# The last block product of a SwiGLU FFN with tokens as rows: residual and LayerNorm along the row, four tiles of 128 tokens

## The chip, the cores and the metric

One core of a Trainium2 chip runs one layer of a diffusion backbone. The metric is the device time of one execution in microseconds; the kernel before took 1520.83 us (median of three runs, 1520.49 to 1521.16). TensorE multiplies and transposes into PSUM, which has eight banks of 128 x 512 float32 values. VectorE (DVE) and ScalarE (ACT) read PSUM and SBUF, GpSimd (POOL) only SBUF, and SyncE (SP) issues most DMA transfers.

## The reference

All is float32. Ahead of the end, the layer computes modulated inputs, a windowed and a global attention, their merge, a first LayerNorm, and the up projection with its convolution and gate. The end, which the change rewrites, is the last two lines:

```
u = silu(gate) * val                       # 1024 tokens x 2816
y = u @ w_down                             # 2816 x 1024
x = alpha * x + gate2 * y                  # gate2: one factor per channel
mu  = mean(x, channels); var = mean((x - mu)^2, channels)
out = (x - mu) * rsqrt(var + 1e-5) * ln2_g + ln2_b
```

The mean and the variance of a token run over its 1024 channels; `gate2`, `ln2_g` and `ln2_b` belong to channels.

## The kernel before, in words

**Layout.** Channels lie on partitions: `zv(f, s)` is the tile of channels 128f to 128f+127 (f = 0 to 7) for a range `s` of tokens, and holds the residual `alpha * x`, to which the gated products are added. Sums over channels are then sums over partitions, which TensorE makes by a product with a column of ones (`onec`).

**Products.** Every float32 operand is split into a high and a low part; `mm3` issues three matmuls (high x high, low x high, high x low). The up and the down projection go by Strassen-Winograd's seven block products instead of eight. For the down projection, tokens 0 to 511 (`h0`) and 512 to 1023 (`h1`) and the two halves of channels and of the inner dimension are the blocks. `product(p)` makes the products p = 1, 6, 2, 7, 4, 5 in that order, each 4 blocks x 11 steps x 3 matmuls of 128 x 512 columns. `ev` and `accum` bring each result from PSUM into `zv`, with the factor `gain` (the gate, or its negative `nmod`).

**The last product, p = 3**, touches only channels 0 to 511 of tokens 512 to 1023. Its operands are the pairs `d3[k]` (k = 0 to 10): `[:, 0]` holds 512 columns of a weight combination, `[:, 1]` the 512 tokens of `h1`, each in a high part `h` and a low part `l`. `last_mm` makes it channel block by channel block with the weights stationary and tokens moving, 256 tokens at a time: first tokens 512 to 767 (`LN2_S[1]`), then 768 to 1023 (`LN2_S[2]`), 4 channel blocks each, so every matmul has 256 columns.

**The norm.** Tokens 0 to 511, and again 512 to 767, go through `ln_steps`: sums and squares by TensorE, the statistics, a broadcast by transposes (`cast`), and then per channel block `apply` and `emit2`, which stores the tile. `pend` holds these steps, and `tick` lets one out when enough matmuls have been issued. The last 256 tokens go another way: `prep` makes squares and `ln2_g`-scaled copies on ScalarE, and `tok(f)` issues on TensorE the sums of z, the transposes that bring channel block f of each 128 tokens into rows (`zt`), and the sums of squares. After the last `tok`, VectorE makes mean and variance (`mvl`, `rsl`, with a power on POOL), puts the mean on (L1813), then scale and shift (L1821; one of the four tiles by ScalarE and POOL, L1818 and L1819), and SP stores four tiles.

**What sets the order.** From the first LayerNorm on, TensorE's order is that of the program (`manual_schedule`); on the other engines a scheduler places instructions, save for VectorE after `win` is entered. A PSUM tile with the tag of an older one waits until the older one has been read. `yb` and `ab` are the two groups of four banks: `ab` holds the results of p = 5, `yb` is free by then.

**Output.** The output is `(8, 128, 1024)`, block, channel, token; for the last 256 tokens the rows are written as 512-byte pieces that hold 128 channels of one token, and the host puts these in place.

Of the kernel before, what the change touches and what calls it, by code (L numbers as in the profile page):

```python
# [70 lines left out]
def layer_kernel(  # L71
# [1659 lines left out]
    s = LN2_S[-1]
    w = s.stop - s.start
    nt = w // P

    def pst(n, name):
        return ps4.tile([P, HALF], F32, tag=f"r{n}", name=name)

    pr = [ht(f"pr{n}", (P, 4, w)) for n in range(4)]
    nc.vector.tensor_scalar(out=pr[0][:, 3, 0:P], in0=ident, scalar1=ln2c[:, 3:4], scalar2=None, op0=ALU.mult)
    nc.gpsimd.tensor_scalar(out=lnr[0], in0=lnr[0], scalar1=-1.0, scalar2=0.0, op0=ALU.mult, op1=ALU.add)  # L1740
    zt = {1: [pst(n, f"zt1_{n}") for n in ab[0:2]]}
    st = pst(ab[2], "stl")
    zero4 = post.tile([P, 8], F32, tag="zero4", name="zero4")
    nc.vector.memset(zero4, 0.0)

    def prep(f):
        nc.scalar.activation(pr[2 + f // 4][:, f % 4], zv(f, s), AF.Square)
        if f != 3:
            nc.scalar.activation(pr[f // 4][:, f % 4], zv(f, s), AF.Identity, scale=ln2c[:, f:f + 1])

    def tok(f):
        z, g = zv(f, s), pr[f // 4][:, f % 4]
        if f == 4:
            nc.tensor.matmul(st[:, 0:2 * nt], ident, zero4[:, 0:2 * nt], start=True, stop=True)
        for t in range(nt):
            ts = slice(t * P, (t + 1) * P)
            nc.tensor.matmul(st[:, t:t + 1], z[:, ts], onec, start=False, stop=True, skip_group_check=True)
        for t in range(nt):
            ts = slice(t * P, (t + 1) * P)
            o = zt[f // 4][t][:, (f % 4) * P:(f % 4 + 1) * P]  # L1760
            if f == 3:
                nc.tensor.matmul(o, z[:, ts], pr[0][:, 3, 0:P], start=True, stop=True)
            else:
                nc.tensor.transpose(o, g[:, ts], ident)
        for t in range(nt):
            ts = slice(t * P, (t + 1) * P)
            nc.tensor.matmul(st[:, nt + t:nt + t + 1], pr[2 + f // 4][:, f % 4, ts], onec, start=False, stop=True,
                             skip_group_check=True)
# [20 lines left out]
    zt[0] = [pst(n, f"zt0_{n}") for n in yb[0:2]]  # L1789
    pend += ln_steps(zs2, zq2, r, "b1", emit2, *LN2_E, LN2_P[1])  # L1790
    r = LN2_S[2]
    for f, done_ in enumerate(((7,), (0,), (1,), (2, 3))):
        o = pst(yb[2 + f % 2], f"yl{f}_{r.start}")[:, 0:w]
        last_mm(o, f, r, range(NH))
        accum(f, r, o, True)
        prep(f)
        for n in done_:
            tok(n)
# [2 lines left out]
    mv, m2, rs = sv
    drain(OTK)
    win = ctx.enter_context(ExitStack())
    win.enter_context(tc.manual_schedule(engines={mybir.EngineType.DVE}))
    nc.vector.tensor_scalar(out=mv, in0=st[:, 0:2 * nt], scalar1=1.0 / D, scalar2=None, op0=ALU.mult)
    nc.vector.tensor_tensor(out=m2[:, 0:nt], in0=mv[:, 0:nt], in1=mv[:, 0:nt], op=ALU.mult)
    nc.vector.scalar_tensor_tensor(out=rs[:, 0:nt], in0=mv[:, nt:2 * nt], scalar=LN_EPS, in1=m2[:, 0:nt],
                                   op0=ALU.add, op1=ALU.subtract)
    nc.gpsimd.tensor_tensor(out=rs[:, 0:nt], in0=rs[:, 0:nt], in1=mhalf[:, 0:nt], op=ALU.pow)
    ot = {}  # L1810
    for t, a in OTO:
        o = ot[t, a] = ht(f"ot{t}_{a}", (P, HALF))
        nc.vector.scalar_tensor_tensor(out=o, in0=lnr[0][:, a], scalar=mv[:, t:t + 1], in1=zt[a][t], op0=ALU.mult,  # L1813
                                       op1=ALU.add)
    for t, a in OTO:
        o = ot[t, a]
        if (t, a) in OTP:
            nc.scalar.activation(o, o, AF.Identity, scale=rs[:, t:t + 1])  # L1818
            nc.gpsimd.tensor_tensor(out=o, in0=o, in1=lnr[1][:, a], op=ALU.add)  # L1819
        else:  # L1820
            nc.vector.scalar_tensor_tensor(out=o, in0=o, scalar=rs[:, t:t + 1], in1=lnr[1][:, a], op0=ALU.mult,  # L1821
                                           op1=ALU.add)
        ts = slice(s.start + t * P, s.start + (t + 1) * P)
        nc.sync.dma_start(out[4 * a:4 * a + 4, :, ts].rearrange("f p q -> p f q"),
                          o.rearrange("p (f q) -> p f q", q=P))
# [89 lines left out]
def _assemble(got):  # L1915
    import numpy as np

    got = np.asarray(got)
    s = LN2_S[-1].start
    r = np.empty((T, KT, P), got.dtype)  # L1920
    r[:s] = got[:, :, :s].transpose(2, 0, 1)
    r[s:] = got[:, :, s:].reshape(KT, P, -1, P).transpose(2, 1, 0, 3).reshape(T - s, KT, P)
# [19 lines left out]
```

## Time and profile before

| | |
|---|---|
| median of three runs | 1520.83 us |
| profiled execution | 1520.56 us |
| its span | 1518.7 us |
| mean granted clock of TensorE | 0.997 |
| TensorE busy | 1500.7 us, 99% |
| VectorE busy | 1166.4 us, 77% |
| ScalarE busy | 789.0 us, 52% |
| GpSimd busy | 757.3 us, 50% |
| first matmul of p = 3 | 1467.05 us from the span's start |
| last matmul's end | 1509.08 us |
| VectorE's last instruction's end | 1514.42 us |

The span runs from the first to the last recorded event; the time of an execution lies 1.86 us above it here. A timeline row gives the start, the duration, the engine, the line, the operation, output and inputs, shapes, and how many are merged; in brackets stand the idle time before it and what ended that. A float32 matmul that is no transpose shows two rows. A matmul's row is longer than the distance to the next, since they are pipelined: the distance is what it costs.

### The profile page before, as it was taken

How to read it: one execution, taken by the hardware profiler on the slowest of the kernel's cores; microseconds unless marked ns; L12 is line 12 of the kernel's file. 1: busy time of each engine (PE TensorE's matmuls, PEld its weight loads, DVE VectorE, ACT ScalarE, POOL GpSimd, SP SyncE). 2: the span in 40 equal slices, each digit the busy share in tenths (PEclk: the TensorE clock that was granted, in tenths of full speed). 3: DMA queues.
4: the chain of work that ended last, by engine and by line, in shares of the span. 5: the costliest groups of instructions: out<-in, count | busy, mean ns of one | idle time of the engine just before them, and what ended most of it. 6: DMA issues, size and time to landing. Idle time of an engine off the chain costs nothing.

```text
span 1518.7 us, 22145 instructions
## 1 busy us (share of the span) xinstructions
PE 1500.7 (99%) x7790; PEld 1260.7 (83%) x7790; DVE 1166.4 (77%) x1755; ACT 789.0 (52%) x1312; POOL 757.3 (50%) x726
## 2 busy tenths in 40 slices
PE   8999999999999999999999999999999999999997
PEld 7888888888988888887888998888888888888887
DVE  7677986538988787777865788888888887557884
ACT  6322222449988677666324555444444444435552
POOL 0356522417766777765234346666667763111121
PEclk9999999999999999999999999999999999999998
DMA  9877662312234576643541322333344448996721
GB/s 370 276 239 244 210 251 86 119 65 69 67 108 116 130 163 166 163 112 97 208 153 49 101 73 98 112 111 111 111 111 111 112 111 238 343 271 211 257 101 56
DMA packets 114239, 231.57 MB, mean 152 GB/s; under 512 B 13168, under 2 KB 28016, under 8 KB 114032
## 3 DMA queue, kind: packets, MB, share of 16 engines
q1 hardware_dynamic: 98976, 201.56, 39.5%
q0 software_dynamic: 10400, 20.19, 8.7%
q10 hardware_dynamic: 4752, 8.42, 1.5%
q8 instruction: 61, 1.00, 0.3%
q14 instruction: 50, 0.41, 0.1%
HBM read 178.93 MB, written 65.86 MB: 161 GB/s over the span
## 4 chain that ended last, share of the span: by engine, by line
PE 91%; DVE 3%; ACT 2%; DMA 2%; issue 1%; POOL 1%; SPq 0%; DVEq 0%; ACTq 0%; POOLq 0%
PE ptr L610 5%; PE p L91 4%; PE p L93 4%; PE p L92 4%; PE g L91 4%; PE g L93 4%; PE g L92 4%; PE av L633 4%; PE av L634 3%; PE b L91 3%; PE b L92 3%; PE b L93 3%; PE s L502 3%; PE s L503 3%; PE c L91 2%; PE c L92 2%
## 5 line engine op out<-in xcount | busy, mean ns | idle before, releaser
L622 DVE TENSOR_TENSOR ptl<-ptr,pth 128x512 fp32r<-128x512 f32 x195 | 128.0, 684 | 20.4 <-ACT pth L621 17.6
L553 ACT ACTIVATE p<-p,nm 128x1280 f32<-128x1280 f32 (+2 forms) x128 | 139.9, 1094 | 6.5 <-DVE p L551 5.9
L88 DVE TENSOR_TENSOR ld<-rd,hd 128x1024 fp32r<-128x1024 f32 x77 | 94.7, 1249 | 50.1 <-ACT hd L83 47.8
L621 ACT CAST pth<-ptr 128x512 fp32r<-128x512 f32 x195 | 111.5, 591 | 30.2 <-PE ptr L610 28.3
L83 ACT CAST hd<-rd 128x1024 fp32r<-128x1024 f32 x77 | 79.5, 1050 | 81.6 <-PE p L93 51.5
L610 PEld LDWEIGHTS ptr<-identr,pb 128*128 128x128 f32 x944 | 96.4, 140 | 23.6 <-ACT pb L556 2.8
L88 POOL TENSOR_TENSOR wlg<-wg,whg 128x512 fp32r<-128x512 f32 x32 | 48.4, 1521 | 129.2 <-ACT whg L83 122.7
L610 PE MATMUL ptr<-identr,pb 128*128 128x128 f32 x944 | 107.6, 245 | 1.2 <-ACT pb L556 0.6
L633 PE MATMUL av<-pth,VT 128*128 128x512 f32 x236 | 104.0, 441 | 0.3
L91 PE MATMUL p<-hd 128*128 128x512 f32 x264 | 103.2, 391 | 0.0
L93 PE MATMUL p<-hd,ld 128*128 128x512 f32 x264 | 102.7, 389 | 0.0
L92 PE MATMUL p<-ld,hd 128*128 128x512 f32 x264 | 102.7, 389 | 0.0
L91 PE MATMUL g<-hh,whg 128*128 128x512 f32 x256 | 100.0, 390 | 0.0
L93 PE MATMUL g<-hh,wlg 128*128 128x512 f32 x256 | 99.7, 389 | 0.0
L92 PE MATMUL g<-hl,whg 128*128 128x512 f32 x256 | 99.6, 389 | 0.0
L634 PE MATMUL av<-ptl,VT 128*128 128x512 f32 x236 | 97.5, 413 | 0.5 <-POOL ptl L88 0.2
L551 DVE TENSOR_SCALAR_CACHE_REDUCE p<-s,cvt,nmc 128x1024 f32<-128x1024 f32 x64 | 84.2, 1316 | 5.1 <-PE s L503 5.1
L502 PE MATMUL s<-KL,q 128*128 128x512 f32 (+2 forms) x192 | 73.5, 383 | 1.4 <-DVE p L551 0.9
L503 PE MATMUL s<-KL,q 128*128 128x512 f32 (+2 forms) x192 | 71.8, 374 | 0.0
L83 ACT CAST wS<-s 128x512 fp32r<-128x512 f32 x76 | 45.3, 621 | 49.8 <-POOL s L1242 49.0
L789 ACT ACTIVATE sg<-g,bgc 128x512 f32<-128x512 f32 x32 | 22.0, 687 | 94.5 <-PE g L93 89.7
L83 ACT CAST wA<-ru 128x512 fp32r<-128x512 f32 x57 | 35.5, 623 | 61.8 <-PE d L93 33.6
(437 smaller groups left out, 4854.6 us busy)
## 6 DMA issues: line engine op xcount, KB each, us to landing
wml<-in_wmodT_dram SPq DMA_DIRECT2D x48, 512.0 KB
ru<-in_w_up_dram SPq DMA_DIRECT2D x38, 512.0 KB
rd<-td SPq DMA_DIRECT2D x55, 256.0 KB
rd<-sd SPq DMA_DIRECT2D x44, 256.0 KB
rd<-in_w_dn_dram SPq DMA_DIRECT2D x33, 256.0 KB
wm<-in_wmodT_dram SPq DMA_DIRECT2D x16, 512.0 KB
wg<-in_w_g_dram SPq DMA_DIRECT2D x32, 256.0 KB
sgd<-sg ACTq DMA_DIRECT2D x32, 256.0 KB
```

What stands on the lines that cost most here:

```text
L83: nc.scalar.copy(hi, src)
L88: lo_eng.tensor_tensor(out=lo, in0=src, in1=hi.bitcast(F32), op=ALU.subtract)
L91: nc.tensor.matmul(ps, a[0], b[0], start=start, stop=False, skip_group_check=resumed)
L92: nc.tensor.matmul(ps, a[0], b[1], start=False, stop=False, skip_group_check=resumed)
L93: nc.tensor.matmul(ps, a[1], b[0], start=False, stop=stop, skip_group_check=resumed)
L502: nc.tensor.matmul(o, self.q[0][:, hs], ks, start=True, stop=False)
L503: nc.tensor.matmul(o, self.q[1][:, hs], ks, start=False, stop=stop)
L553: nc.scalar.activation(row, row, AF.Exp, bias=self.nm[:, hs], scale=-1.0, accum_out=self.sm[:, hs])
L610: i = nc.tensor.transpose(tr[:, h * P:(h + 1) * P], self.bits[:, h, n * P:(n + 1) * P], identr)
L622: nc.vector.tensor_tensor(out=lo, in0=tr, in1=hi.bitcast(F32), op=ALU.subtract)
L633: nc.tensor.matmul(self.av, v, hi, start=first, stop=False)
L634: nc.tensor.matmul(self.av, v, lo, start=False, stop=self.left == 0)
```

## The change

Product p = 3 is turned round. `last_mm(t, ks)` makes, for 128 tokens t (0 to 3), the rows `rows[t, 0]` of one bank: the tokens are stationary, 512 channels move. `turn(t)` transposes the eight tiles of z of these tokens into two more banks, `rows[t, 1]` (channels 0 to 511) and `rows[t, 2]` (512 to 1023). `finish_rows(t)` lets VectorE multiply the product by the gate row `grow`, add `rows[t, 1]`, take mean and variance with BN_STATS and BN_AGGR, and put mean, scale and shift on along the row; a power on POOL is left. `grow` is the negative gate, spread over the partitions by four transposes (`gps`) and copied from PSUM by ScalarE. The first seven steps of tiles 0 and 1 are issued ahead of it; tiles 2 and 3 are turned after six steps. `prep`, `tok`, the second `ln_steps` and the sums of tokens 512 to 767 go. Tiles 0 to 2 are stored whole by SP; of tile 3 SP stores the first half and ScalarE's queue the second, in rows of 2 KB. The output is now flat: 1024 channels by 512 tokens, then 512 tokens by 1024 channels.

```
 evict: p == 5
                 accum(f + 4, h1, o, False)
-                sums(f + 4, LN2_S[1], f == 0)
...
-    r = LN2_S[1]
-    yl = [pst(n, f"yl{f}")[:, 0:w] for f, n in enumerate(yb)]
-    for f in range(4):
-        last_mm(yl[f], f, r, range(len(D3AT)))
-    for f in range(4):
-        last_mm(yl[f], f, r, range(len(D3AT), NH))
-        accum(f, r, yl[f], True)
-        sums(f, r, False)
-        prep(f + 4)
-        if f:
-            tok(f + 3)
...
-    pend += ln_steps(zs2, zq2, r, "b1", emit2, *LN2_E, LN2_P[1])
-    r = LN2_S[2]
-    for f, done_ in enumerate(((7,), (0,), (1,), (2, 3))):
...
+    def rbank(t, a):
+        n = ((yb[0], yb[1], ab[2], ab[3]), (yb[2], ab[0]), (yb[3], ab[1]))[a]
+        rows[t, a] = ps4.tile([P, HALF], F32, tag=f"r{n[t % len(n)]}", name=f"rw{a}_{t}")
+        return rows[t, a]
+
+    def last_mm(t, ks):
+        q = slice(t * P, (t + 1) * P)
+        if (t, 0) not in rows:
+            rbank(t, 0)
         for k in ks:
             h, l = d3[k]
-            mm3(o, (h[:, 0, c], l[:, 0, c]), (h[:, 1, q], l[:, 1, q]), k == 0, k == NH - 1)
+            mm3(rows[t, 0], (h[:, 1, q], l[:, 1, q]), (h[:, 0], l[:, 0]), k == 0, k == NH - 1)
+            tick(HALF / 0.8)
+
+    def turn(t):
+        for a in (1, 2):
+            o = rbank(t, a)
+            for n in range(4):
+                z = zv(n + 4 * a - 4, slice(HALF + t * P, HALF + (t + 1) * P))
+                nc.tensor.transpose(o[:, n * P:(n + 1) * P], z, ident)
+
+    def finish_rows(t):
+        end = t == NE - 1
...
+        nc.vector.bn_stats(out=bs[:, 1], in_=rows[t, 2])
+        nc.vector.tensor_tensor(out=o[:, 0], in0=rows[t, 0], in1=grow, op=ALU.mult)
+        nc.vector.tensor_tensor(out=o[:, 0], in0=rows[t, 1], in1=o[:, 0], op=ALU.add)
+        nc.vector.bn_stats(out=bs[:, 0], in_=o[:, 0])
+        nc.vector.bn_aggr(out=mv, in_=bs)
+        nc.vector.tensor_scalar(out=rs, in0=mv[:, 1:2], scalar1=LN_EPS, scalar2=None, op0=ALU.add)
+        nc.gpsimd.tensor_tensor(out=rs, in0=rs, in1=mhalf[:, 0:1], op=ALU.pow)
+        for a in (0, 1):
+            nc.vector.scalar_tensor_tensor(out=o[:, a], in0=rows[t, 2] if a else o[:, 0], scalar=mv[:, 0:1],
+                                           in1=lnr[0][:, a], op0=ALU.subtract, op1=ALU.mult)
+        for a in (0, 1):
+            nc.vector.scalar_tensor_tensor(out=o[:, a], in0=o[:, a], scalar=rs, in1=lnr[1][:, a],
+                                           op0=ALU.mult, op1=ALU.add)
+            if end:
+                (nc.scalar if a else nc.sync).dma_start(rows_out[t][:, a * HALF:(a + 1) * HALF], o[:, a])
+        if not end:
+            nc.sync.dma_start(rows_out[t], o.rearrange("p a q -> p (a q)"))
+
+    n = len(D3AT)
+    for t in (0, 1):
+        last_mm(t, range(n))
+    drain()
+    gps = ps4.tile([P, HALF], F32, tag=f"r{yb[2]}", name="gps")
+    for f in range(4):
+        nc.tensor.transpose(gps[:, f * P:(f + 1) * P], nmod[:, f:f + 1].to_broadcast([P, P]), ident)
+    nc.scalar.copy(grow, gps)
+    win = ctx.enter_context(ExitStack())
+    for t in (0, 1):
+        turn(t)
+        last_mm(t, range(n, NH))
+        finish_rows(t)
+    for t in (2, 3):
+        last_mm(t, range(6))
+        turn(t)
+        last_mm(t, range(6, NH))
+        if t == NE - 1:
+            win.enter_context(tc.manual_schedule(engines={mybir.EngineType.DVE}))
+        finish_rows(t)
```

In the built programs, TensorE's last instructions were, before, the end of block 3's product and the last two `tok`s (`yl` is the product's bank, `stl` the sums, `zt` the rows, `pr` the squares and scaled copies):

```order
L91 MATMUL yl_768_14897<-hd_10_14490 128x256
L92 MATMUL yl_768_14897<-ld_10_14491,hd_10_14490 128x256
L93 MATMUL yl_768_14897<-hd_10_14490,ld_10_14491 128x256
L1757 MATMUL stl<-onec,zz_1_12956 128x1 x2
L1764 MATMUL zt_4_14709<-ident,pr_14515 128x128
L1764 MATMUL zt_5_14710<-ident,pr_14515 128x128
L1767 MATMUL stl<-onec,pr_14517 128x1 x2
L1757 MATMUL stl<-onec,zz_1_12958 128x1 x2
L1762 MATMUL zt_4_14709<-pr_14515,zz_1_12958 128x128
L1762 MATMUL zt_5_14710<-pr_14515,zz_1_12958 128x128
L1767 MATMUL stl<-onec,pr_14517 128x1 x2
```

Such rows now stand nowhere; TensorE ends with products of `rw_3`, and the transposes come between products. On TensorE now, after the first seven steps of tiles 0 and 1 (`rw_0`, `rw_1` are the tiles `rows`; lines are those of the changed kernel):

```order
L89 MATMUL rw_1_14525<-hd_6_14231,ld_6_14232 128x512
L1779 MATMUL gps<-ident,nmod 128x128 x4
L1747 MATMUL rw_0_14553<-ident,zz_1_12952 128x128
L1747 MATMUL rw_0_14553<-ident,zz_1_12954 128x128
L1747 MATMUL rw_0_14553<-ident,zz_1_12956 128x128
L1747 MATMUL rw_0_14553<-ident,zz_1_12958 128x128
L1747 MATMUL rw_0_14558<-ident,zz_1_12952 128x128
L1747 MATMUL rw_0_14558<-ident,zz_1_12954 128x128
L1747 MATMUL rw_0_14558<-ident,zz_1_12956 128x128
L1747 MATMUL rw_0_14558<-ident,zz_1_12958 128x128
L87 MATMUL rw_0_14503<-hd_7_14469 128x512
```

`gps` and `rw_0_14553` share bank yb[2]. VectorE's last instructions were, before:

```order
L1618 SCALAR_TENSOR_TENSOR zz_1_12958<-yl_768_14897,nmod,zz_1_12958 128x256
L1805 TENSOR_SCALAR mvl<-stl 128x4
L1806 TENSOR_TENSOR m2l<-mvl 128x2
L1807 SCALAR_TENSOR_TENSOR rsl<-mvl,m2l 128x2
L1813 SCALAR_TENSOR_TENSOR ot_0_14959<-lnr,mvl,zt_4_14709 128x512
L1813 SCALAR_TENSOR_TENSOR ot_1_14961<-lnr,mvl,zt_7_14521 128x512
L1813 SCALAR_TENSOR_TENSOR ot_0_14963<-lnr,mvl,zt_5_14710 128x512
L1813 SCALAR_TENSOR_TENSOR ot_1_14965<-lnr,mvl,zt_6_14522 128x512
L1821 SCALAR_TENSOR_TENSOR ot_1_14961<-ot_1_14961,rsl,lnr_12950 128x512
L1821 SCALAR_TENSOR_TENSOR ot_0_14963<-ot_0_14963,rsl,lnr_12950 128x512
L1821 SCALAR_TENSOR_TENSOR ot_1_14965<-ot_1_14965,rsl,lnr_12950 128x512
```

and are now, from the last row of tile 2 on:

```order
L1766 SCALAR_TENSOR_TENSOR ot_14676<-ot_14676,rsr_14675,lnr_12950 128x512 x2
L1755 BN_STATS bs_14735<-rw_3_14713 128x6
L1756 TENSOR_TENSOR ot_14738<-rw_3_14689,grow 128x512
L1757 TENSOR_TENSOR ot_14738<-rw_3_14708,ot_14738 128x512
L1758 BN_STATS bs_14735<-ot_14738 128x6
L1759 BN_AGGR mvr_14736<-bs_14735 128x2
L1760 TENSOR_SCALAR rsr_14737<-mvr_14736 128x1
L1763 SCALAR_TENSOR_TENSOR ot_14738<-ot_14738,mvr_14736,lnr 128x512
L1763 SCALAR_TENSOR_TENSOR ot_14738<-rw_3_14713,mvr_14736,lnr 128x512
L1766 SCALAR_TENSOR_TENSOR ot_14738<-ot_14738,rsr_14737,lnr_12950 128x512 x2
```

The mean is taken from the rows themselves instead of `stl`, and four wide instructions stand at the end as seven did before. Tiles 0 to 2 stand ahead of these rows, each whole before the next, but for the BN_STATS of tile 1's upper half, which stands inside tile 0.

More of the change, by code (lines that the diff above doesn't have):

```diff
@@ L41 @@
 LN2_D = 5000.0, 4000.0, 1500.0, 700.0
-LN2_E = 3500.0, 3000.0, 800.0, 500.0
 NCL = 3
-LN2_S = slice(0, 512), slice(512, 768), slice(768, 1024)
 S1 = 0, 1
@@ L52 @@
 RAWB = 3
-OTP = (0, 0),
-OTO = (0, 0), (0, 1), (1, 0), (1, 1)
-OTK = 4
 PSU = 6, 7, 2, 3, 4, 5, 0, 1
@@ L58 @@
 UE = "vector", "vector", "vector", "vector", "vector", "gpsimd", "gpsimd"
-LN2_P = 2, 2, 2
 GAP = 1
@@ L78, in layer_kernel @@
     nc = tc.nc
+    rows_out = out[D * HALF:].rearrange("(t q c) -> t q c", q=P, c=D)
+    out = out[0:D * HALF].rearrange("(f p q) -> f p q", p=P, q=HALF)
     PSUM = bass.MemoryType.PSUM
@@ L1715, in ev @@
                 accum(f + 4, h1, o, False)
-                sums(f + 4, LN2_S[1], f == 0)
         evict += [lambda f=f, o=acc[f]: ev(f, o) for f in range(4)]
         if p == 4:
-            after.append(lambda: pend.extend(ln_steps(zs2, zq2, h0, "b0", emit2, *LN2_D, LN2_P[0])))
+            after.append(lambda: pend.extend(ln_steps(zs2, zq2, h0, "b0", emit2, *LN2_D)))
     yb, ab = sides[nside[0] % 2], sides[nside[0] % 2 ^ 1]
-    banks[:] = [ab[3]]
     d3 += [dload(3, k, ring) for k in range(len(D3AT), NH)]
@@ L1728, in layer_kernel @@
         accum(f, h1, acc[f], True)
[L1731 to L1768, printed above, removed]
@@ L1770, in last_mm @@
-    def last_mm(o, f, r, ks):
-        q = slice(r.start - HALF, r.stop - HALF)
-        c = slice(f * P, (f + 1) * P)
+    NE = 4
+    grow = post.tile([P, HALF], F32, tag="grow", name="grow")
+    rows = {}
+    def rbank(t, a):
[6 more added lines that the diff above has]
+            rbank(t, 0)
@@ L1789, in layer_kernel @@
-    zt[0] = [pst(n, f"zt0_{n}") for n in yb[0:2]]
-    pend += ln_steps(zs2, zq2, r, "b1", emit2, *LN2_E, LN2_P[1])
-    r = LN2_S[2]
-    for f, done_ in enumerate(((7,), (0,), (1,), (2, 3))):
[L1793 to L1798, printed above, removed]
-    hput(*[f"{a}d3_{k}" for k in range(len(D3AT)) for a in "hl"])
-    sv = [post.tile([P, 2 * nt], F32, tag=f"{n}l", name=f"{n}l") for n in ("mv", "m2", "rs")]
@@ L1801, in layer_kernel @@
[L1801 to L1825, printed above, removed]
+            mm3(rows[t, 0], (h[:, 1, q], l[:, 1, q]), (h[:, 0], l[:, 0]), k == 0, k == NH - 1)
@@ new lines, in last_mm @@
+            tick(HALF / 0.8)
[7 more added lines that the diff above has]
+        end = t == NE - 1
+        bs = post.tile([P, 2, 6], F32, tag="bs", name=f"bs{t}", bufs=2)
+        mv = post.tile([P, 2], F32, tag="mvr", name=f"mvr{t}", bufs=2)
+        rs = post.tile([P, 1], F32, tag="rsr", name=f"rsr{t}", bufs=2)
+        o = ht(f"ot{t}", (P, 2, HALF))
+        nc.vector.bn_stats(out=bs[:, 1], in_=rows[t, 2])
[15 more added lines that the diff above has]
+            nc.sync.dma_start(rows_out[t], o.rearrange("p a q -> p (a q)"))
@@ L1918, in _assemble @@
     got = np.asarray(got)
[L1919 to L1922, printed above, removed]
+    r = np.empty((T, D), got.dtype)
+    r[:HALF] = got[:D * HALF].reshape(D, HALF).T
+    r[HALF:] = got[D * HALF:].reshape(T - HALF, D)
     return r.reshape(1, T, D)
@@ L1936 @@
         args[name] = nc.dram_tensor(f"in_{name}_dram", a.shape, _mybir.dt.from_np(a.dtype), kind="ExternalInput").ap()
-    out = nc.dram_tensor("out_0_dram", (KT, P, T), _mybir.dt.float32, kind="ExternalOutput").ap()
+    out = nc.dram_tensor("out_0_dram", (D * T,), _mybir.dt.float32, kind="ExternalOutput").ap()
     with _tile.TileContext(nc) as tc:
```

1 line of the change is left out of this document (removed).

## The prediction

> **What bounds the kernel now.** I read the page's head and its chain of waits first, then the stretch that the change rewrites, cut in two: TensorE's share of it and what follows its last matmul.
>
> ```profile
> span 1518.7 us, 22145 instructions
> PE 91%; DVE 3%; ACT 2%; DMA 2%; issue 1%; POOL 1%; SPq 0%; DVEq 0%; ACTq 0%; POOLq 0%
> ```
> ```profile
> 1467.05:1509.10 42.05, 42.03 (x361) 41.94 (x359) 22.86 (x50) 15.87 (x36) 4.07 (x6) 1.00 0.13 44
> 1509.10:1518.70 9.60, 0.00 (x0) 0.00 (x0) 5.23 (x10) 0.72 (x1) 1.96 (x2) 0.52 0.40 110
> ```
>
> The columns after the length are busy time and instruction count of PE, PEld, DVE, ACT and POOL, then granted clock, DMA share and GB/s. TensorE never rests for 42.05 us (the other engines have slack there), then 9.60 us pass without it. So I price two things: TensorE's queue from 1467.05 on, and the tail behind its last matmul. Everything ahead of 1467.05 keeps its instructions.
>
> **TensorE, what goes.** The timeline of TensorE shows one `tok` among the 256-column products:
>
> ```profile
> 1482.48 0.28 PE L92 MATMUL yl<-ld,hd 128*128 128x256 f32 x1
> 1482.60 0.28 PE L93 MATMUL yl<-hd,ld 128*128 128x256 f32 x1
> 1482.72 0.50 PE L1757 MATMUL stl<-onec,zz 128*128 128x1 f32 x4
> 1483.08 0.42 PE L1764 MATMUL zt<-ident,pr 128*128 128x128 f32 x2
> 1483.34 0.50 PE L1767 MATMUL stl<-onec,pr 128*128 128x1 f32 x4
> 1483.70 0.36 PE L91 MATMUL yl<-hd 128*128 128x256 f32 x1
> 1483.90 0.28 PE L92 MATMUL yl<-ld,hd 128*128 128x256 f32 x1
> ```
>
> Starts of products lie 0.12 us apart; 264 of them (2 parts x 4 blocks x 11 x 3) are 31.7 us. A `tok` takes 1483.70 - 1482.72 = 0.98 us, and the first product behind it 0.20 instead of 0.12: 1.06, eight times 8.5 us. What is left of 42.05, 1.85 us, is the third piece: statistics and broadcast of the normalization of tokens 512 to 767, the zero seed, the longer block-3 multiplications. All three go.
>
> **TensorE, what comes.** There are 4 x 11 x 3 = 132 products of 512 columns, 32 transposes of z and 4 of the gate column. Their rows are those of the product before, around its broadcast:
>
> ```profile
> 1455.73 0.39 PE L93 MATMUL p<-hd,ld 128*128 128x512 f32 x1
> ...
> 1456.41 0.39 PE L93 MATMUL p<-hd,ld 128*128 128x512 f32 x1
> 1456.63 0.60 PE L1207 MATMUL bcrb<-ident,rsb 128*128 128x128 f32 x4
> 1457.07 0.60 PE L1207 MATMUL bcmb<-ident,mrb 128*128 128x128 f32 x4
> 1457.42 0.47 PE L91 MATMUL p<-hd 128*128 128x512 f32 x1
> 1457.74 0.39 PE L92 MATMUL p<-ld,hd 128*128 128x512 f32 x1
> ```
>
> Three products in 0.68 us are 0.227 each: 132 make 30.0 us. A plain transpose of real data (L1764 above) costs 0.13: 32 make 4.2. The lower price is the eight broadcast ones, 0.79 / 8 = 0.10, which would make 3.2; I take 0.13, the same form. Each of four groups pays 0.32 - 0.227 = 0.09 on the way back to products: 0.4. The four gate transposes are 0.44.
>
> One wait is added. `grow` is copied from bank yb[2] by ScalarE, and the next TensorE instruction, the first transpose of `turn(0)`, writes that bank. Everything of the end is queued behind it. The like copy is
>
> ```profile
> 1457.70 0.59 ACT L1210 COPY mbb<-bcmb 128x512 f32<-128x512 f32 x1 [1.18 <-PE bcmb L1207]
> ```
>
> It starts 0.03 behind the transposes' end (1457.07 + 0.60) and ends at 1458.29, where TensorE could have gone on at 1457.42: 0.87, with the way back to TensorE 0.9 us. Below it can hardly lie under the copy's own 0.59; above I bound it by the longest TensorE wait for ScalarE that the trace has, 2.5 us (row further down). The eight `accum`s that `turn(0)` also needs are not late:
>
> ```profile
> 1470.61 2.06 DVE L1618 SCALAR_TENSOR_TENSOR zz<-p,modc,zz 128x512 f32<-128x512 f32 x3
> ```
>
> Spaced 0.66 (2.06 less one row's 0.74, over two), without the sums between them, they end by 1476; the 42 products ahead of the gate's transposes last until 1467.05 + 9.5 = 1476.6.
>
> Sum: 30.0 + 4.2 + 0.4 + 0.4 + 0.9 = 35.9 us for 42.05: **6.2 us less**. TensorE issues its last product by 1502.9 and, a 0.39-us row spaced 0.227, ends it at 1503.1.
>
> **VectorE's tail.** Before and after, this is what follows the last matmul:
>
> ```profile
> 1509.12 0.16 DVE L1805 TENSOR_SCALAR mvl<-stl 128x4 f32<-128x4 f32 x1 [1.82 <-PE stl L1767]
> 1509.32 0.16 DVE L1806 TENSOR_TENSOR m2l<-mvl 128x2 f32<-128x2 f32 x1
> 1509.62 2.72 DVE L1813 SCALAR_TENSOR_TENSOR ot<-lnr,mvl,zt 128x512 f32<-128x512 f32 x4
> 1509.75 0.70 POOL L1809 TENSOR_TENSOR rsl<-rsl,mhalf 128x2 f32<-128x2 f32 x1 [5.99 <-DVE rsl L1807]
> 1512.26 2.16 DVE L1821 SCALAR_TENSOR_TENSOR ot<-ot,rsl,lnr 128x512 f32<-128x512 f32 x3
> 1512.58 2.32 SPq L1824 DMA_DIRECT2D out_dram<-ot  x4
> ```
>
> VectorE ends at 1514.42, 5.3 us behind TensorE. The new tail, of the last 128 tokens alone: gate product and residual sum (both out of PSUM), BN_STATS, BN_AGGR, the epsilon, then four SCALAR_TENSOR_TENSOR; the BN_STATS of the other half has run before. From grouped lines:
>
> ```profile
> L1215 DVE TENSOR_TENSOR zz<-zz,bcrb 128x512 f32<-128x512 f32 x8 | 5.1, 678 | 0.0
> L1153 DVE TENSOR_TENSOR zs<-zs,z 128x512 f32<-128x512 f32 x3 | 2.1, 688 | 0.0
> L364 DVE TENSOR_REDUCE cvt<-sqq 128x8 f32<-128x512 f32 x8 | 5.4, 681 | 3.0 <-ACT sqq L357 3.0
> L841 DVE TENSOR_SCALAR bias_qa<-bias_qa 128x512 f32<-128x512 f32 x1 | 0.4, 418 | 0.0
> ```
>
> A dependent successor starts 0.04 behind (1509.28 to 1509.32), so product and sum are 0.72 each. BN_STATS is not in this trace. The nearest row is the reduction over 512 elements, 0.68; below it the fastest 512-element row, 0.42; above it two such reductions, 1.36. I take 0.72 with its gap. BN_AGGR (not in the trace either; 0.68 at most, as the wide reduction) and epsilon are 0.2 each, as the small rows are spaced; the four wide ones 2.72, as L1813. The power on POOL, 0.70, is hidden under the first two wide ones (1.3); uncovered it would cost 0.7. Sum with the start: 0.04 + 0.72 + 0.72 + 0.72 + 0.4 + 2.72 = 5.3 us. **No change**, -0.3 to +0.7.
>
> [...]
>
> **The output.** Half-microsecond slices around the last store, and around an earlier store of 2-KB rows:
>
> ```profile
> 1462.50:1463.00 0.50, 0.50 (x4) 0.40 (x3) 0.50 (x2) 0.50 (x2) 0.36 (x1) 1.00 1.01 381
> 1513.50:1514.00 0.50, 0.00 (x0) 0.00 (x0) 0.50 (x2) 0.00 (x0) 0.00 (x0) 0.50 0.94 251
> 1516.50:1517.00 0.50, 0.00 (x0) 0.00 (x0) 0.00 (x0) 0.00 (x0) 0.00 (x0) 0.50 1.10 291
> 1517.00:1517.50 0.50, 0.00 (x0) 0.00 (x0) 0.00 (x0) 0.00 (x0) 0.00 (x0) 0.50 0.38 103
> ```
>
> Now four 256-KB stores in 512-byte pieces leave in a bunch: data from about 1513.5 (0.9 behind the first issue) to 1517.2, the engines full, then 1.5 us to the span's end. That is 4.28 us behind VectorE. After the change two 256-KB halves in 2-KB pieces are left, 0.66 us apart, on two queues; the 512 KB of the tile before left some 8 us earlier. For the last half: 0.9 + 256 KB at 377 to 381 GB/s = 0.7 + 1.5 = 3.1 us. **1.2 us less**; no gain if ScalarE's queue is slower by as much, 0.3 more if the rest shrinks.
>
> **Sum.** 1503.1 + 5.3 + 3.1 = 1511.5, 7.2 us under 1518.7. The profiled execution took 1520.56 us with what lies around its span, so 1513.4; the median of the runs is 0.27 above that execution: **1513.6 us**. Cheaper ends (transposes -1.0, wait -0.3, tail -0.3, store -0.3) give 1511.7, dearer ones (wait +1.6, tail +0.7, store +1.2) 1517.1. All seldom meet: the forecast's own range is 1511.7 to 1516.5.
>
> **Rivals.**
>
> *TensorE's clock drops at the wait (slower).*
>
> ```profile
> PE q1acc L313 <- ACT hh L233: 2.5, 1, 2.5
> ```
> ```profile
> 1506.62 0.50 PE L1757 MATMUL stl<-onec,zz 128*128 128x1 f32 x4
> ...
> 1508.58 0.50 PE L1767 MATMUL stl<-onec,pr 128*128 128x1 f32 x4
> ```
> ```profile
> 8.00:9.00 1.00, 0.00 (x0) 0.00 (x0) 0.54 (x1) 0.93 (x3) 0.00 (x0) 1.00 1.03 406
> 1509.50:1509.60 0.10, 0.00 (x0) 0.00 (x0) 0.09 (x1) 0.00 (x0) 0.00 (x0) 0.72 0.00 0
> ```
>
> For it: the clock leaves 1.00 within 0.5 us of the last matmul at 1509.08, less than the 0.9 that I expect for `grow`. Behind that wait stand 90 products and 32 transposes, 25 us; at half clock to the end they take 25 more: 1539. It decides from the wait whose following rows show 0.5. Against it: TensorE waited 2.5 us around the slice at 8 to 9, with a granted 1.00, and the drop at 1509.5 came behind the last two `tok`s, 2.5 us with many one-column matmuls. [...]
>
> *VectorE becomes the bound.* A tile costs it 0.72 x 4 (product, sum, two BN_STATS) + 0.4 + 2.72 = 6.0 us against TensorE's 33 x 0.227 + 8 x 0.13 + 0.09 = 8.6. The tightest bank is yb[3]: read last 4.7 us into `finish_rows(0)`, wanted by `turn(2)` 1.1 + 2.7 + 4.1 = 7.9 us in. BN_STATS would have to cost 2.0 us (1.3 more, twice) to fill a tile's 8.6; then the tail alone is 1.3 longer: 1514.9 and more.
>
> *It does not pay.* Only TensorE's order is written by hand; a scheduler could put the row arithmetic late, so that tiles 0 to 2 are still open when tile 3 is ready. One extra tile behind the last product, 6 us, and a fuller output queue, 1.2, take all 7.2 back: 1520.8. Against it: on VectorE the tiles stand in sequence in the new order, with 2.6 us of slack each.
>
> **How the numbers follow.** Forecast 0.84; clock 0.04; VectorE the bound 0.07; no gain 0.05. A measurement here tells about 0.2% (3 us) from no change. The forecast and the late VectorE lie beyond that: faster 0.91; same 0.05; slower 0.04. The range takes in the dearer ends and a one-tile wait: 1511.2 to 1517.0.
>
> **What would show it.** TensorE's last matmul near 1503; 512-column rows 0.227 apart; one idle of about 0.9 before `turn(0)`, put down to ScalarE's copy, and none at the other three; BN_STATS near 0.7; VectorE's end 5.3 behind TensorE's; 3.1 from there to the span's end. The prediction fails on a granted clock under 1.00 before 1503, TensorE waits with VectorE as releaser, or a tail over 10 us.

## The result, and the profile after

The changed kernel takes **1513.1 us** (median of six runs, 1512.6 to 1514.5) against 1520.8 for the kernel before in the same session (six runs, 1519.9 to 1522.2): a ratio of 0.995, with a 95% interval of 0.9937 to 0.9963. The forecast was 1513.6 us. The profiled execution took 1512.96 us and spans 1511.1.

The head of the page, the totals of the engines and the chain of waits, as shown of the kernel before:

```profile
span 1511.1 us, 21688 instructions
PE 1493.9 (99%) x7598; PEld 1248.4 (83%) x7598; DVE 1172.3 (78%) x1745; ACT 775.1 (51%) x1280; POOL 746.9 (49%) x721
PE 92%; DVE 3%; ACT 2%; issue 1%; DMA 1%; POOL 1%; SPq 0%; DVEq 0%; ACTq 0%; POOLq 0%
```

The bound is still TensorE's queue and then a tail. The same stretch in three pieces (first product of tile 0 to TensorE's end, VectorE's tail, the output; columns as in the prediction):

```profile
1466.85:1501.88 35.03, 34.35 (x169) 28.31 (x167) 26.10 (x42) 2.96 (x5) 2.90 (x3) 1.00 0.18 68
1501.88:1507.13 5.25, 0.00 (x0) 0.00 (x0) 5.08 (x9) 0.00 (x0) 0.92 (x1) 0.82 0.00 0
1507.13:1511.10 3.97, 0.00 (x0) 0.00 (x0) 0.00 (x1) 0.00 (x0) 0.00 (x0) 0.50 0.37 134
```

TensorE's piece was 42.05 before and is 35.03; VectorE's was 5.3 and is 5.25; the output's was 4.28 and is 3.97. The clock was granted in full (1.00) through all of TensorE's piece.

The one wait and two of the four groups of transposes, on TensorE's timeline, with the copy on ScalarE's:

```profile
1476.37 0.60 PE L1779 MATMUL gps<-ident,nmod 128*128 128x128 f32 x4
1477.64 1.09 PE L1747 MATMUL rw<-ident,zz 128*128 128x128 f32 x8 [0.68 <-ACT grow L1780]
1478.49 0.48 PE L87 MATMUL rw<-hd 128*128 128x512 f32 x1
1478.81 0.39 PE L88 MATMUL rw<-ld,hd 128*128 128x512 f32 x1
...
1489.02 1.03 PE L1747 MATMUL rw<-ident,zz 128*128 128x128 f32 x8
1489.81 0.48 PE L87 MATMUL rw<-hd 128*128 128x512 f32 x1
```
```profile
1477.00 0.59 ACT L1780 COPY grow<-gps 128x512 f32<-128x512 f32 x1 [7.78 <-PE gps L1779]
```

From the gate's transposes to the first of tile 0 pass 1477.64 - 1476.37 = 1.27 us, 0.40 of them the transposes themselves and 0.87 the wait. Eight transposes then take 0.85 (1477.64 to 1478.49), and 0.79 where nothing is waited for (1489.02 to 1489.81): 0.10 each. Way back: 1478.81 - 1478.49 = 0.32, as predicted.

VectorE's tail and the two stores, from the timeline of all engines:

```profile
1501.92 0.69 DVE L1756 TENSOR_TENSOR ot<-rw,grow 128x512 f32<-128x512 f32 x1 [2.58 <-PE rw L89]
1502.64 0.69 DVE L1757 TENSOR_TENSOR ot<-rw,ot 128x512 f32<-128x512 f32 x1
1503.37 0.69 DVE L1758 BATCH_NORM_STATS2 bs<-ot 128x6 f32<-128x512 f32 x1
1504.10 0.21 DVE L1759 BATCH_NORM_AGGREGATE mvr<-bs 128x2 f32<-128x12 f32 x1
1504.34 0.15 DVE L1760 TENSOR_SCALAR rsr<-mvr 128x1 f32<-128x1 f32 x1
1504.41 0.74 DVE L1763 SCALAR_TENSOR_TENSOR ot<-ot,mvr,lnr 128x512 f32<-128x512 f32 x1
1504.64 0.92 POOL L1761 TENSOR_TENSOR rsr<-rsr,mhalf 128x1 f32<-128x1 f32 x1 [7.49 <-DVE rsr L1760]
1505.07 0.74 DVE L1763 SCALAR_TENSOR_TENSOR ot<-rw,mvr,lnr 128x512 f32<-128x512 f32 x1
1505.73 1.40 DVE L1766 SCALAR_TENSOR_TENSOR ot<-ot,rsr,lnr 128x512 f32<-128x512 f32 x2
1506.50 0.33 SPq L1769 DMA_DIRECT2D out_dram<-ot  x1
1507.16 0.34 ACTq L1769 DMA_DIRECT2D out_dram<-ot  x1
```

BN_STATS costs 0.69 us, as much as the product and the sum ahead of it. The power on POOL ends at 1505.56, before L1766 asks for it at 1505.73.

The output, in half-microsecond slices, and the DMA queues between VectorE's end and the span's end (packets, MB, share of 16 DMA engines):

```profile
1507.50:1508.00 0.50, 0.00 (x0) 0.00 (x0) 0.00 (x0) 0.00 (x0) 0.00 (x0) 0.50 1.03 381
1508.00:1508.50 0.50, 0.00 (x0) 0.00 (x0) 0.00 (x0) 0.00 (x0) 0.00 (x0) 0.50 1.03 377
1508.50:1509.00 0.50, 0.00 (x0) 0.00 (x0) 0.00 (x0) 0.00 (x0) 0.00 (x0) 0.50 0.50 180
1509.00:1509.50 0.50, 0.00 (x0) 0.00 (x0) 0.00 (x0) 0.00 (x0) 0.00 (x0) 0.50 0.06 12
```
```profile
DMA packets 289, 0.53 MB, mean 134 GB/s; under 512 B 32, under 2 KB 32, under 8 KB 288
q10 hardware_dynamic: 144, 0.26, 18.3%
q1 hardware_dynamic: 144, 0.26, 18.0%
q14 instruction: 1, 0.01, 0.6%
```

The bulk is through by 1508.9; then a thin stream follows at a share of 0.06, one sixteenth, so one DMA engine of 16. And there is a 289th packet, one of 8 KB on an instruction queue (q14), between the stores. No term of the prediction stands for it. By the trace's single packets it starts at 1508.69 and takes 0.41 us; behind it come, one after the other, the store's last three packets of 2 KB, at 1509.10, 1509.18 and 1509.36, which take 0.08, 0.19 and 0.22 us where 0.09 is usual.

The pieces add up to a hit, but two of its terms missed and cancelled: TensorE's piece came out 1.0 us shorter than predicted, the output 0.9 longer.

### The profile page after: what moved, and what is told of

The parts are those of the page before. It is cut to its first block, busy times and chain, and to the rows that moved or that the text cites. A ratio compares the mean times of both kernels' runs of the same rounds, so it can differ in the third digit from the quotient of the medians.

```text
span 1511.1 us, 21688 instructions
## 1 busy us (share of the span) xinstructions
PE 1493.9 (99%) x7598; PEld 1248.4 (83%) x7598; DVE 1172.3 (78%) x1745; ACT 775.1 (51%) x1280; POOL 746.9 (49%) x721
## 4 chain that ended last, share of the span: by engine, by line
PE 92%; DVE 3%; ACT 2%; issue 1%; DMA 1%; POOL 1%; SPq 0%; DVEq 0%; ACTq 0%; POOLq 0%
PE ptr L606 5%; PE p L87 4%; PE p L88 4%; PE p L89 4%; PE g L87 4%; PE g L89 4%; PE g L88 4%; PE av L629 4%; PE av L630 3%; PE b L87 3%; PE b L88 3%; PE b L89 3%; PE s L498 3%; PE s L499 3%; PE q1acc L309 3%; PE c L87 2%
```

## The experiments

The theory: the end is a plain sum of TensorE's queue, VectorE's tail and the store, and each piece can be moved alone by the amount its rows give. Its rivals are those of the prediction (the clock, VectorE as the bound) and, for the late store, ScalarE's queue against the instruction packet. A single execution is no measure of a microsecond here, since the part ahead of the change ends anywhere from 1466.3 to 1468.0 us in most of these traces (1470.2 in one); so single executions are compared by pieces of the end, as in the three rows above.

**The wait for `grow`.** The gate's transposes go to another bank, so that `turn(0)` need not wait until ScalarE has read them.

```
-    gps = ps4.tile([P, HALF], F32, tag=f"r{yb[2]}", name="gps")
+    gps = ps4.tile([P, HALF], F32, tag=f"r{ab[0]}", name="gps")
```

> Only the bank of the gate transposes changes: ab[0] instead of yb[2], so the first transposes of turn(0) no longer write the bank that ScalarE still reads. Theory (the 0.68 us idle before turn(0) is this bank conflict and nothing else): the idle vanishes, TensorE's stretch from the first product of the rows to the end of the last falls from 35.0 to 34.3-34.4 us, the span by 0.6-0.7. Rival (turn(0) would wait for z at that place anyway, or TensorE stands for the copy at another place): a wait of about the same length with VectorE as releaser, or one at turn(1); stretch 35.0.

```profile
1467.85:1501.99 34.14, 34.13 (x169) 28.34 (x167) 26.11 (x42) 2.98 (x5) 2.91 (x3) 1.00 0.18 70
```

TensorE never rests; its piece is 0.89 us shorter than 35.03. The predicted 0.9 for this wait holds. (The 0.6 to 0.7 expected just above was the idle time of 0.68, which counts from the modelled end of a row, later than the next one could have started.) The execution as a whole took 1512.97 us, no less than the changed kernel, because tile 0 happened to begin 1.0 later.

**The width of a product.** Tiles 2 and 3 make their products as two halves of 256 columns (`half_mm`, whose definition is left out here, makes all eleven steps of one half).

```
-        last_mm(t, range(6))
+        half_mm(t, slice(0, 256))
         turn(t)
-        last_mm(t, range(6, NH))
+        half_mm(t, slice(256, HALF))
```

> Edit: tiles 2 and 3 make their last block product as two halves of 256 channels, one after the other in the same bank, with the transposes of the residual between the halves; tiles 0 and 1 and all of VectorE's work stay. The same sums are computed, by 132 products of 256 columns in place of 66 of 512. Theory (the 30.0-us term of the sum, 512 columns at 0.227 a product against 0.12 for 256, carries the gain): TensorE's stretch from the first product of tile 0 to its last end grows by 66 x (2 x 0.12 - 0.227) = 0.9 us, from 35.0 to 35.9, and nothing else moves. Rival (a product of 256 columns with 128 tokens stationary pays for its weights, since a load now serves half as many columns): more than 2 us longer, 37 or above. Rival (width is worth nothing): 35.0.

```profile
1470.23:1506.05 35.82, 35.14 (x235) 31.98 (x233) 26.11 (x42) 2.97 (x5) 2.90 (x3) 1.00 0.17 66
11.00:14.00 3.00, 3.00 (x9) 2.35 (x8) 3.00 (x5) 1.52 (x3) 0.00 (x0) 0.50 1.04 420
```

35.82 is 0.79 above 35.03, where 0.87 was worked out. Width is worth 0.79 / 66 = 0.012 us per product of 512 columns, 1.6 of the 7 us for all 132; the rest of TensorE's gain is, by the rows and not by a run of its own, the eight `tok`s and the broadcast that went, less what came. (The execution took 1517.08: tile 0 began 3.4 late. At 6.5 to 9.4 us TensorE waited 2.82 us for ScalarE, where the changed kernel waited 1.77, and then its clock stood at half through all of 11.00 to 14.00, as the second line shows. The longer wait makes 1.05 of the 3.4, and these 3.00 us of work at half clock 1.5, an estimate from that line: 2.5 at least, at a place which the edit does not touch.)

**The clock behind a wait.** ScalarE copies the gate row 14 times, 13 of them for nothing, so that TensorE's wait grows from 0.68 to 8.69 us.

```
-    nc.scalar.copy(grow, gps)
+    for _ in range(14):
+        nc.scalar.copy(grow, gps)
```

> ScalarE copies the gate rows fourteen times instead of once, so TensorE waits before turn(0) some 7 to 8.5 us instead of 0.68. It prices the rival of the prediction in which the clock falls at this wait. Theory (the clock falls in a long enough wait and comes back within a few us of work): granted clock 0.50 at the end of the wait, products 0.45 us apart for up to 3.5 us, then 0.227 again; TensorE's stretch 35.0 + 7.5 + 1.7 = 44 us. Rival (it stays at half to the end, as the prediction priced it): 35.0 + 7.5 + 25 = 67 us. If the clock does not fall even here: 42.5.

Timeline of TensorE, and slices with the granted clock (the third number from the right):

```profile
1485.06 1.97 PE L1747 MATMUL rw<-ident,zz 128*128 128x128 f32 x8 [8.69 <-ACT grow L1781]
```
```profile
1478.00:1478.50 0.50, 0.00 (x0) 0.00 (x0) 0.00 (x0) 0.47 (x2) 0.00 (x0) 1.00 0.00 0
1478.50:1479.00 0.50, 0.00 (x0) 0.00 (x0) 0.00 (x0) 0.47 (x2) 0.00 (x0) 0.87 0.00 0
1479.00:1479.50 0.50, 0.00 (x0) 0.00 (x0) 0.00 (x0) 0.47 (x2) 0.00 (x0) 0.50 0.00 0
...
1488.50:1489.00 0.50, 0.50 (x3) 0.37 (x2) 0.00 (x0) 0.00 (x0) 0.00 (x0) 0.50 0.00 0
1489.00:1489.50 0.50, 0.50 (x4) 0.41 (x3) 0.00 (x0) 0.00 (x0) 0.00 (x0) 0.89 0.00 0
1466.25:1511.20 44.95, 36.26 (x169) 29.94 (x167) 26.10 (x42) 10.57 (x18) 2.90 (x3) 0.89 0.14 53
```

TensorE stops at 1485.06 - 8.69 = 1476.37. The clock is whole for 2.5 us, then halves, and is whole again about 4.0 us after work resumes. The piece is 44.95 - 35.03 = 9.92 longer, 8.01 of it the longer wait: the half clock cost **1.9 us**, about half of the 4.0 us for which it met work, and not the 25 that the slower rival put on it. Neither 2.5 nor 4.0 need be a constant. In the records of the granted clock, the stretch at half is 10.24 us in this run and the one at full clock behind it 27.3: as 3 to 8, in steps of 10.24 / 3 = 3.413 us. The one stretch at full clock is 1498.45 us in the changed kernel and 1505.28 in the one before, 6.83 apart, which is two such steps. That the clock changed only at points such a step apart, and that how long it outlived a stop depended on where the stop fell between two of them, is inferred from these four stretches and not shown by a run of its own.

**VectorE's slack.** Tiles 0 to 2 take their second BN_STATS twice, and in another kernel four times; the result is the same.

```
-        nc.vector.bn_stats(out=bs[:, 0], in_=o[:, 0])
+        for _ in range(1 if end else 2):
+            nc.vector.bn_stats(out=bs[:, 0], in_=o[:, 0])
```

> Edit: tiles 0 to 2 take their second BN_STATS twice, same result; VectorE has 3 x 0.7 = 2.1 us more to do ahead of tile 3. VectorE was idle 0.50 us ahead of tile 2 and 2.58 ahead of tile 3 after the change, 3.1 in all. Theory A (VectorE's slack is one sum over the tiles, 3.1 us): 2.1 fits, tile 3's gate product still starts within 0.1 us of TensorE's end, and VectorE ends 5.2 to 5.3 behind it. Theory B (slack is bounded tile by tile; tile 2's is only 0.5): TensorE or tile 3 is late by 0.7 to 1.6 us. Prediction on record (2.6 us each): no change, as A.

> Tiles 0 to 2 run their second BN_STATS four times instead of once: three more of 0.69 us, each on the same output, so about 2.2 us more per tile and 6.5 in all; the result stays. By the prediction's own words (2.6 us of slack in each tile): no change, VectorE's last tile starts when TensorE ends. Rival (tiles 0 and 1 reach VectorE 3.6 us apart, so slack is one sum of 3.1 us for all three tiles: 0.50 before tile 2 and 2.58 before tile 3): the gate product of tile 3 starts 3.3-3.5 us later against TensorE's end, the span is 3.3-3.5 us longer, TensorE itself does not wait (stretch 35.0).

The pieces, first of the run with twice, then of the run with four times:

```profile
1467.26:1502.30 35.04, 34.36 (x169) 28.32 (x167) 28.00 (x45) 2.96 (x5) 2.90 (x3) 1.00 0.16 63
1502.30:1507.55 5.25, 0.00 (x0) 0.00 (x0) 5.08 (x9) 0.00 (x0) 0.92 (x1) 0.77 0.09 34
```
```profile
1467.99:1503.29 35.30, 34.56 (x169) 28.30 (x167) 29.26 (x48) 2.97 (x5) 2.37 (x3) 1.00 0.14 53
1503.29:1510.54 7.25, 0.00 (x1) 0.00 (x0) 7.11 (x13) 0.00 (x0) 1.45 (x2) 0.74 0.18 73
```

In the changed kernel VectorE waits for TensorE like this ahead of tile 2 (the row ahead of tile 3 stands above), and closes tile 2 with the second row:

```profile
1493.51 0.69 DVE L1756 TENSOR_TENSOR ot<-rw,grow 128x512 f32<-128x512 f32 x1 [0.50 <-PE rw L89]
...
1497.33 1.40 DVE L1766 SCALAR_TENSOR_TENSOR ot<-ot,rsr,lnr 128x512 f32<-128x512 f32 x2
```

The wait is 0.50 us, and 2.58 ahead of tile 3: 3.1 in all. Three repetitions add 28.00 - 26.10 = 1.90 us of work and move nothing. Nine add 29.26 + 7.11 - 26.10 - 5.08 = 5.19; less 3.1 leaves 2.1, and TensorE's piece and the tail together are 0.27 + 2.00 = 2.27 longer. So the slack is one sum. The 0.27, where none was expected, lies among the eight transposes of `turn(2)`: the fifth, the first into bank yb[3], starts 0.34 us behind the fourth in place of 0.11, at 1490.85, and VectorE reads that bank for tile 0 until 1490.70. It is the bank that the prediction called the tightest. The 3.3 to 3.5 expected there was too much because a repeated BN_STATS costs 0.58 in the mean, not the 0.72 of one that waits for its forerunner. Ahead of tile 2 there is little slack because tiles 0 and 1 come close together: seven steps of each were made beforehand, so tile 1 costs TensorE only 0.8 + 0.09 + 12 x 0.227 = 3.6 us, less than VectorE's 6 a tile.

**The late store: ScalarE's queue?** The last half is stored by SP too.

```
-                (nc.scalar if a else nc.sync).dma_start(rows_out[t][:, a * HALF:(a + 1) * HALF], o[:, a])
+                nc.sync.dma_start(rows_out[t][:, a * HALF:(a + 1) * HALF], o[:, a])
```

> Only the queue of the last half tile's store changes: SP instead of ScalarE's queue. In the changed kernel 3.97 us pass from VectorE's end to the span's end where 3.1 were forecast; nearly all data have landed 1.6 us after VectorE's end, then one DMA engine's worth of bytes trickles until 1509.5. Theory A (ScalarE's queue is the cause: its store confirms late, or an instruction load of ScalarE's program shares a DMA engine with it): from VectorE's end to the span's end 3.0-3.2 us, no trickle behind the data. Rival B (a 2-KB-row store confirms that late whichever queue issues it): 3.9-4.0 us as now. TensorE's stretch stays 35.0.

```profile
1506.81:1511.00 4.19, 0.00 (x0) 0.00 (x0) 0.00 (x0) 0.00 (x0) 0.00 (x0) 0.50 0.35 127
```

4.19 in place of 3.97: the queue is not the cause. But in the run with nine more BN_STATS the same piece was 3.16, and its packet on q14 lay far ahead of the stores. That gave a new theory: the packet loads VectorE's instructions (it moves when VectorE has more of them), and holds up what one DMA engine has of the last store.

**The late store: the packet?** Nine small VectorE instructions, read by nobody, are put early into VectorE's queue, once alone and once with the other gate bank; and the changed kernel is run again.

```
+    pad = post.tile([P, 8], F32, tag="pad", name="pad")
+    for _ in range(9):
+        nc.vector.memset(pad, 0.0)
```

> Edit: the gate's transposes go to bank ab[0] instead of yb[2], so that turn(0) needn't wait for ScalarE's copy; and nine tiny VectorE instructions (8 columns of zeros into a tile of their own that nobody reads) are put early into VectorE's queue, well ahead of the end. The computation stays whole. Theory: the copy's wait goes (stretch 35.0 to 34.1), and the 8-KB packet on the instruction queue, which after the change lies in the last store's window and in the run with nine more VectorE instructions lay 5 us before VectorE's end, comes 4 to 6 us earlier than VectorE's end; then the last store is not held up: 3.1 to 3.2 us from VectorE's end to the span's end in place of 3.97, with no thin stream of data at the end. In all 0.9 + 0.8 = 1.7 us less than the changed kernel: about 1511.4. Rival (the packet on the instruction queue has nothing to do with the thin stream): 3.9 to 4.2 from VectorE's end, 1512.2. Rival (it is another engine's instruction stream): the packet stays within 1 us of VectorE's end, and the tail is 3.9 to 4.2.

> The changed kernel once more, beside the two below on one chip. Theory: as before, packet of the instruction queue inside the last store's window, 3.9 to 4.2 us from VectorE's end to the span's end, TensorE's stretch 35.0; median 1512.5 to 1514.0. If the late end of the store were chance and not the packet, this run could as well show 3.1.

> Edit: the changed kernel with the nine small early VectorE instructions and nothing else (the gate's transposes stay in bank yb[2]). The computation stays whole. Theory: TensorE's wait for ScalarE's copy stays (0.68 idle, stretch 35.0), VectorE's tail stays at 5.25, and the packet of the instruction queue comes 4 us or more ahead of VectorE's end, so that the store ends 3.1 us behind it: 0.85 us less than the changed kernel. Rival (the earlier gate bank, and not the small instructions, moved the packet): the packet stays in the store's window and the end at 3.9 to 4.2.

With the nine instructions alone, the DMA queues and the last pieces are:

```profile
DMA packets 288, 0.52 MB, mean 168 GB/s; under 512 B 32, under 2 KB 32, under 8 KB 288
q1 hardware_dynamic: 144, 0.26, 23.1%
q10 hardware_dynamic: 144, 0.26, 22.7%
```
```profile
1467.29:1502.32 35.03, 34.35 (x169) 28.32 (x167) 26.09 (x42) 2.97 (x5) 2.90 (x3) 1.00 0.18 68
1502.32:1507.58 5.26, 0.00 (x1) 0.00 (x0) 5.08 (x9) 0.00 (x0) 0.92 (x1) 0.74 0.00 0
1507.58:1510.70 3.12, 0.00 (x0) 0.00 (x0) 0.00 (x1) 0.00 (x0) 0.00 (x0) 0.50 0.46 168
```

The 289th packet is gone from the window (it lies at 1500.0 to 1500.5), the thin stream with it, and the store takes 3.12: the predicted 3.1. Of all twelve profiles with the new end, by the half-microsecond slice in which the packet lies, counted from VectorE's end:

| kernel | packet, us from VectorE's end | VectorE's end to span's end |
|---|---|---|
| changed kernel | +1.4 | 3.97 |
| the same again | +1.3 | 4.00 |
| gate bank | +1.3 | 3.95 |
| store by SP | +1.7 | 4.19 |
| half width | +1.2 | 3.99 |
| 14 copies | +1.5 | 3.94 |
| BN_STATS twice | -1.1 | 3.15 |
| BN_STATS four times | -5.5 | 3.16 |
| nine instructions | -7.6 | 3.12 |
| nine, and gate bank | -7.9 | 3.12 |
| the same, last tile split | -8.1 | 3.09 |
| the same again | -7.8 | 3.14 |

Six with the packet among the stores: 3.94 to 4.19. Six with it ahead: 3.09 to 3.16. (The page gives a span to 0.1 us, so the last column is good to 0.05.) That its place costs 0.8 to 0.9 us is shown; the store by SP, at 4.19, has no run beside it without the packet. That it loads VectorE's instructions is inferred: it moves by 2.5 us with three more of them, by 6.9 to 9.5 with nine or more, and not with one store fewer on ScalarE's queue or 13 more copies there. The count fits: in all twelve traces the packet starts when VectorE has begun 1745 to 1747 of the instructions that the page counts, early or late. In the changed kernel these are all it has (x1745). Of the delay, 0.41 us is the packet itself and 0.23 the two slow ones behind it; why these are slow, and what the rest is, stays open.

In medians the effect is near what five runs resolve. The nine instructions alone took 1512.47 us (1511.4 to 1514.2) beside 1512.52 (1512.3 to 1513.3) for the changed kernel in the same session, where 0.85 less was expected: not seen. Tile 0 began at 1467.29 in the one profile and at 1466.41 in the other; whether the small instructions cost that much ahead of the end or chance did is not settled. With the gate bank as well it was 1511.26 (1510.7 to 1514.1) in another session, near the 1511.4 expected, with TensorE's piece at 34.14 and the store at 3.12, as expected.

**A shorter last tile.** On top of the gate bank and the nine instructions, tile 3 is turned first and its product made in two halves in two banks, so that VectorE works on the first under the second (the definition of `half_mm`, the third set of statistics and the branch for tile 2 are left out).

```
+        if t == 3:
+            turn(t)
+            halves = [ps4.tile([P, HALF], F32, tag=f"r{n}", name=f"rh{n}")[:, 0:256] for n in (ab[3], yb[0])]
+            for n, o in enumerate(halves):
+                half_mm(t, o, slice(256 * n, 256 * n + 256))
...
+            for n, c in enumerate((slice(0, 256), slice(256, HALF)) if end else (slice(0, HALF),)):
```

> Edit: as the run with the gate in bank ab[0] and nine small early VectorE instructions, and besides tile 3 is turned first and its product made in two halves of 256 channels in two banks, so that VectorE puts gate, residual and BN_STATS on the first half while TensorE makes the second; three sets of statistics are aggregated. The computation stays whole. Theory: TensorE 33 x (0.24 - 0.227) = 0.4 us longer; behind its end VectorE has 3 rows of 256 columns (0.4 us each by half of 0.7 plus a gap) in place of three of 512: tail 5.25 to 4.3 or 4.4; net 0.4 to 0.5 less than without the split, about 1511.0. Rival (short rows cost as much as long ones): tail 5.2, net 0.4 longer.

> The version with the gate in bank ab[0], nine small early VectorE instructions and tile 3 in two halves, once more beside the changed kernel. Theory: stretch 34.55, VectorE's tail 4.5, store 3.1: 42.15 us from the first product of tile 0 to the span's end against 44.25 for the changed kernel, so 2.1 us less in the median, about 1511; if the 2.4 us between the medians seen so far came from the chip and not from the kernel, the two medians would lie within 0.5 us.

The pieces in the second of these runs:

```profile
1467.23:1501.78 34.55, 34.55 (x202) 30.19 (x200) 27.18 (x45) 2.96 (x5) 2.90 (x3) 1.00 0.18 69
1501.78:1506.26 4.48, 0.00 (x0) 0.00 (x0) 4.30 (x9) 0.00 (x0) 0.92 (x1) 0.80 0.00 0
1506.26:1509.40 3.14, 0.00 (x0) 0.00 (x0) 0.00 (x1) 0.00 (x0) 0.00 (x0) 0.50 0.45 167
```

TensorE pays 0.41 and VectorE's tail falls from 5.26 to 4.48: 0.37 less in all, a little under the 0.4 to 0.5 expected, since a row of 256 costs 0.46 with its gap and not 0.4. The end takes 42.17 us against the changed kernel's 44.25. In the same session the medians are **1511.0 us** (1510.2 to 1511.6) and 1512.5 (1512.3 to 1513.3); beside the kernel before its ratio is 0.9933 (0.992 to 0.9945). It is the best version found, 1.5 us under the changed kernel where the pieces made 2.1, with runs that do not overlap. Its first run, in another session, had a median of 1510.65.

## Why the prediction was right, and where its terms were not

- **Reading of the bound: right.** The gain came where it was put, in TensorE's queue: 7.0 us of the 7.6 in span, the other 0.6 are the store (0.3), tile 0's earlier start (0.2) and VectorE's tail (0.1).
- **TensorE's products: right.** 0.227 apart, and the price of width stood up to the half-width run (0.79 for 0.87).
- **"32 make 4.2": mis-sized by 1.0.** Eight transposes take 0.79 to 0.80: 32 make 3.2. The prediction had both prices, 0.13 from a pair of transposes that stand between one-column matmuls, and 0.10 from a run of eight. It went by the likeness of the operands ("the same form"), but real data in a run of eight cost as much as the broadcast columns had. By single records the transposes start 0.109 apart in both places; the first of the pair, behind a one-column matmul, costs 0.144, while a product follows the last of eight by 0.03. So the neighbours decide.
- **The wait: right.** Releaser, place and size (0.87 on the timeline, 0.89 by taking it away); the three other groups waited for nothing.
- **VectorE's tail: right**, 5.25 for 5.3. BN_STATS, taken from a reduction at 0.68, measured 0.69; BN_AGGR 0.21 for 0.2. The power cost 0.92 instead of 0.70, which its cover hid with 0.17 to spare.
- **The store: "0.9 + 256 KB at 377 to 381 GB/s = 0.7 + 1.5 = 3.1": mis-sized by 0.9.** The sum is right for a store with no such packet in its window (3.09 to 3.16 in six profiles), and so is each term, near enough: 0.90, 0.83 and 1.38 in the last of them. An instruction packet in its window was left out. The trace of the kernel before has such a packet too, between 1510.5 and 1511.0, ahead of its last stores' data at 1513.5, so it cost nothing there; that its place would move with the instruction count was the thing to ask.
- **The clock as a rival: its place was possible, its price far too high.** A wait of 0.87 did not bring the clock down (1.00 through all of TensorE's piece), and one of 8.7 cost 1.9 us beside itself, not 25: the clock was whole again 4.0 us after work resumed. The 1.7 us for the clock, and the half clock of up to 3.5 us, in the expectation of the long wait are terms that no run shows; the run showed 1.9 and 4.0.
- **"2.6 us of slack each": wrong as worded.** It is 3.1 us over all tiles, used up in any of them. The conclusion, that VectorE does not become the bound, stood, with 3.1 to spare.
- **"It does not pay": did not come about.** VectorE had closed tile 2 at 1498.73, 3.1 us ahead of TensorE's end, so one tile alone was left behind the last product.

So the total was right by 0.5 us with two errors of 1.0 and 0.9 of opposite sign: that it came so near was luck. The range would have held without the cancellation: either error alone gives 1512.6 or 1514.5.

## What to carry to other kernels

Price an operation by a row that stands in the same company, not only in the same form: a transpose in a run of eight cost 0.10 us here, and 0.13 next to one-column matmuls. Where a kernel ends in a store, look for instruction packets in its window; moving one by a few instructions was worth 0.8 us in the trace, though five runs of that alone did not show it in the median. The wait of 0.9 us cost only itself, and a bank chosen so that nobody waits for a reader recovered even that.

## What the runs showed of the hardware that was not expected

- An 8-KB packet of an instruction queue among the last store's packets made the store end 0.8 to 0.9 us later, with a sixteenth of the DMA share (0.06) in use meanwhile.
- In the long wait the clock fell 2.5 us after TensorE stopped, and in the twelve profiles with the new end anywhere from about 2.0 us after the last matmul (a mean clock of 0.72 over 4.48 us, in the first run with the last tile split) to 5.2 (1.00 over 5.26, with 14 copies); in the changed kernel it was 3.4 (0.82 over 5.25). The four stretches of the clock above (10.24 and 27.3; 1498.45 and 1505.28, 6.83 apart) fit steps of 3.413 us. In the kernel before, whose last 2.5 us held many one-column matmuls, the clock fell 0.46 us after the last; the records do not say what makes it fall.
- The 8-KB packet started at nearly the same count of VectorE's instructions, 1745 to 1747, in twelve traces in which its place moved by over 9 us against VectorE's end.
- The power on POOL took longer for one column (0.92) than for two (0.70 in the kernel before).
